# Two pairs of gate and up units per SwiGLU by Strassen's seven block products

## The chip, the cores and the metric

The kernel runs on one core of one Trainium2 chip. The metric is the device time of one execution in microseconds (us), the median of several runs. A profile is one execution of its own, with a time of its own.

## What is computed

A decoder trunk of four layers over 256 tokens of width 1024, in fp32. Each layer adds half a SwiGLU, a token mixer with a memory attention, and another half SwiGLU to the stream `x`; so there are eight SwiGLUs.

```python
def rms_norm(x, g):
    xf = x.astype(jnp.float32)
    y = xf * lax.rsqrt(jnp.mean(xf * xf, axis=-1, keepdims=True) + EPS)
    return (y * g.astype(jnp.float32)).astype(x.dtype)

def swiglu(x, wg, wu, wd):
    return (jax.nn.silu(x @ wg) * (x @ wu)) @ wd
...
x += 0.5 * swiglu(rms_norm(x, ffn_norm[i, j]), w_gate[i, j], w_up[i, j], w_down[i, j])
```

`w_gate` and `w_up` are 1024 x 2816, `w_down` is 2816 x 1024.

## The kernel before

The 256 tokens are two tiles of 128 (t = 0 and 1). Each tile is a generator, `chain(t)`, that runs through the layers and takes one unit of weights each time it is sent one. A unit is up to 2 MB of weights. For a gate/up unit ("g") it is 1024 x 512: 256 gate columns beside 256 up columns; a SwiGLU has eleven of them. Its down units ("d") are 512 x 1024 each (the last one is half). `FFN_ORDER` gives the order: four g, then d, then g, g, d and so on. `plan` writes down the units (`self.units`) and the order in which the chains get them (`self.seq`); `both` gives a unit to tile 0 and then to tile 1.

Precision: each fp32 operand is parted into a high part `hi`, which is the operand copied to fp32r, and the rest `lo`. A product is three matmuls of 128x128 by 128x512, hi x hi, hi x lo and lo x hi (`mm3`, lines 228 to 230). A g unit for one tile has eight blocks of K, so 24 matmuls, into one PSUM bank (`project`, tile `pg`). Of a d unit, four blocks of K into two banks, also 24 (tile `acc`).

Weights: `fetch` (line 182) loads a unit by two DMAs of 1 MB on SP's queue into `raw`, which has three buffers. `split` queues four quarters a unit; each is a copy on ScalarE (`hi`, line 200) and a subtraction on VectorE (`lo`, line 201) of 128x1024 elements. `hi` and `lo` have nine buffers each (`HALVES`). `split_some` issues queued quarters, one or two at each `tick`, and all of a unit's before the unit is used. `run` is the loop over `self.seq`; behind each unit it calls `advance`, which fetches the unit three further on and queues the quarters of the one two further on. A tick stands in the middle of a product and after it.

After a g unit, ScalarE takes a tanh of the gate half (line 1070), VectorE makes the product h in two steps (1071, 1076), and two units together are turned by TensorE and parted again (1084 to 1086). The norm is not applied to the tokens ahead of the product: the columns of `x` are turned and multiplied by the gains (`norm_half`, lines 324 to 329), and 1/rms of a token enters as a scale of the product (`norm_stats`, `rstd`, `rh`, `r2`, computed by POOL from a sum of squares of line 336).

Buffers are tiles of tags: `a4` (nine of 4 KB a partition, used by the mixers and by `scr` of `norm_stats`), `a2` (14 of 2 KB), `a1` (ten of 1 KB). PSUM: four banks A (`acc`, mixers), two B (`pg`), two C (`pT`, all turning). The code only says in which order work is issued; a scheduler settles at build time in which order each engine takes it, among what is ready and has a buffer, earlier issued work first, and places the semaphores. Each engine then works in that fixed order.

Of the kernel before, what the change touches and what calls it, by code (L numbers as in the profile page):

```python
# [78 lines left out]
class Net:  # L79
    def __init__(self, ctx, tc, a, layers):  # L80
        self.tc, self.nc, self.a = tc, tc.nc, a
        self.layers = layers

        def pool(name, **k):
            return ctx.enter_context(tc.tile_pool(name=name, bufs=1, **k))

        self.cp, self.wp, self.ap, self.sp = pool("const"), pool("weights"), pool("act"), pool("small")
        self.ps = pool("psum", space=PSUM)
        self.units, self.raw, self.parts = [], {}, {}
        self.n_fetch = self.n_split = 0  # L90
        self.seq, self.due, self.queue, self.memkv = [], [], [[], []], {}
        self.ticks = 0
        self.joint, self.open = [], []
        self.st, self.splits = [{}, {}], []
        self.plan()

# [29 lines left out]
    def plan(self):  # L126
        a = self.a

        def ffn(i, j):
            for kind, u in FFN_ORDER:  # L130
                if kind == "g":
                    self.units.append(("w", [a["gu"][i, j, u, 0], a["gu"][i, j, u, 1]], None))
                elif u < 5:
                    self.units.append(("w", [a["dn"][i, j, 2 * u], a["dn"][i, j, 2 * u + 1]], None))
                else:
                    self.units.append(("w", [a["dn"][i, j, 10]], None))

        def memory(i):
            self.units.append(("w", [a["memT"]], None))
            self.units.append(("w", [a["mkv"][i, 0], a["mkv"][i, 1]], i))  # L140
            self.seq.append((len(self.units) - 2, 2))

        def both(n):
            self.seq += [(n, 0), (n, 1)]

        for j, i in enumerate(self.layers):
            n = len(self.units)
            ffn(i, 0)
            for u in range(n, len(self.units)):
                both(u)  # L150
            if j == 0:
                memory(i)
            kind = i % 3
            names = {0: ["ret"] * 5, 1: ["dsa0", "dsa1", "dsa2", "dsa2"],
                     2: ["nsa0", "nsa0", "nsa0", "nsa1", "nsa2", "nsa3"]}[kind]
# [12 lines left out]
            self.seq += [(n - 2, 0), (n - 1, 0), (n - 2, 1), (n - 1, 1)]  # L168
            ffn(i, 1)
            for u in range(n, len(self.units)):  # L170
                both(u)

    def fetch(self):
        u = self.n_fetch
        if u >= len(self.units):
            return
        self.n_fetch += 1
        self.raw[u] = []
        for ap in self.units[u][1]:
            n = ap.shape[1]  # L180
# [1 line left out]
            self.nc.sync.dma_start(r, ap)  # L182
            self.raw[u].append(r)

    def split(self):

        nc, u = self.nc, self.n_split
        if u >= len(self.units):
            return
        self.n_split += 1  # L190
        self.parts[u] = []
        gain = self.units[u][2]

# [52 lines left out]
    def tick(self):  # L246
# [13 lines left out]

    def push(self, key, t, first, second=None):

        i = len(self.joint)
        while i and self.joint[i - 1][0] > key:
            i -= 1
        self.joint.insert(i, (key, t, first, second))

    def step(self):

        if self.joint and len(self.open) < 2:  # L270
            key, t, first, second = self.joint[0]
# [3 lines left out]
            self.joint.pop(0)  # L275
            first()
            if second is not None:
                self.open.append((t, second))
# [14 lines left out]
    def flush(self, t):  # L293
        due, self.due = self.due, []
        for n, fn, x in due:
            if x in (None, t):
                fn()
            else:
                self.due.append((n, fn, x))
        while any(o[0] == t for o in self.open) or any(j[1] == t for j in self.joint):  # L300
            self.step()
        while self.queue[t]:
            self.queue[t].pop(0)()
# [10 lines left out]
    def norm_half(self, t, g, b, st):  # L314
# [10 lines left out]
        for k in range(4):  # L325
# [3 lines left out]
            nc.vector.scalar_tensor_tensor(lo[:, c], p[:, k], gain, hi[:, c].bitcast(F32),  # L329
                                           op0=OP.mult, op1=OP.subtract)  # L330

    def norm_stats(self, t, st):
# [721 lines left out]
    def ffn(self, t, g, st):  # L1054
# [4 lines left out]
        for kind, ui in FFN_ORDER:  # L1059
            u = yield  # L1060
            if not H:
                s, r, rh, r2 = st["n"]
            if kind == "g":
                if u == 0:
                    p = self.first[t]
                else:
# [3 lines left out]
                nc.scalar.activation(th, p[:, :256], AF.Tanh, scale=rh)  # L1070
# [5 lines left out]
                nc.vector.scalar_tensor_tensor(hs, th, r2, p[:, 256:], op0=OP.mult, op1=OP.mult)  # L1076
# [12 lines left out]
            else:  # L1089
# [4 lines left out]
                for cb in range(2):  # L1094
# [6 lines left out]
                    if nd == 5:  # L1101
# [2 lines left out]
                        if g is None:  # L1104
                            nc.scalar.dma_start(self.a["out"][t * 128:(t + 1) * 128, cb * 512:cb * 512 + 512], xs)
                        else:
                            self.norm_half(t, g, cb, st)
                    if cb == 0:
                        self.tick()
                nd += 1  # L1110
# [19 lines left out]
    def opening(self):  # L1130
# [52 lines left out]
        def gained(t, b, p):  # L1183
            w = self.t2([128, 4, 128], "xg")
            nc.vector.tensor_mul(w, p, self.gains[:, g, 4 * b:4 * b + 4, None].to_broadcast([128, 4, 128]))
            return w

        def parted(t, b, w):
# [4 lines left out]
        def block(k, p):  # L1193
            hi, lo = self.st[0]["s"]
            gain = self.gains[:, g, k:k + 1]
            nc.scalar.activation(hi[:, k], p[:, k], AF.Copy, scale=gain)
            nc.vector.scalar_tensor_tensor(lo[:, k], p[:, k], gain, hi[:, k].bitcast(F32),
                                           op0=OP.mult, op1=OP.subtract)
            halve(k, 1)

        pt = turned(0, 0)
        self.idle(4)
        for k in range(2):
# [33 lines left out]
    def chain(self, t):  # L1237
# [3 lines left out]
        for i in self.layers:  # L1241
# [12 lines left out]
                xs = X[:, cb * 512:cb * 512 + 512]  # L1254
                nc.vector.tensor_add(xs, acc, xs)
            for b in range(2):
                self.norm_half(t, 2 * i + 1, b, st)
            self.norm_stats(t, st)
            yield from self.ffn(t, None if i == self.layers[-1] else 2 * i + 2, st)

    def run(self):
# [40 lines left out]
        for n, (u, t) in enumerate(self.seq):  # L1302
            self.split_some(0, u + 1 if t == 2 else u)
            try:
                chains[t].send(u)
            except StopIteration:
                pass
            self.tick()
# [100 lines left out]
```

## Time and profile before

| | |
|---|---|
| median of 3 runs | 2052.04 us (2051.94 to 2052.83) |
| the profiled execution's own time | 2050.38 us |
| its span, first to last instruction | 2048.6 us |
| TensorE, VectorE, ScalarE, POOL busy | 2029.6, 1250.7, 1015.5, 161.6 us |
| read from HBM | 349.07 MB |

The engines are PE (TensorE's matmuls; PEld is its loading of weights, which overlaps), DVE (VectorE), ACT (ScalarE), POOL (GpSimd) and SP, which only issues DMAs. A SwiGLU takes about 188 us of TensorE, eight of them some 1500 of the 2049 us; between them lie the mixers and the output projections. A matmul's duration in the trace contains its pipeline, so neighbours overlap; the pitch is the distance of starts.

### The profile page before, as it was taken

What the parts mean: (1) busy time and instruction counts of PE and PEld (TensorE: products, weight loads), DVE (VectorE), ACT (ScalarE), POOL (GpSimd) and SP (SyncE); (2) the same over time, 40 slices, a digit from 0 to 9 for tenths busy, and PEclk for the clock granted to TensorE, in tenths of its full rate; (3) what the DMA queues carried; (4) which work ended last, traced back from release to release, by engine and by line L of the source; (5) the groups of instructions that cost most, each with busy time, mean ns of one, the idle gap of its engine ahead of it and who ended that gap; (6) DMA issues with size and microseconds to landing.
All of it is one profiled execution on the core that took longest, in us unless ns stands there. A gap on an engine that the chain in (4) does not pass through costs nothing.

```text
span 2048.6 us, 25033 instructions
## 1 busy us (share of the span) xinstructions
PE 2029.6 (99%) x9662; PEld 1653.0 (81%) x9662; DVE 1250.7 (61%) x1912; ACT 1015.5 (50%) x1494; POOL 161.6 (8%) x285
## 2 busy tenths in 40 slices
PE   9999999999999999999999999999999999999999
PEld 6888777888888887888888877878888888778887
DVE  7556756555655687755665576765556656657553
ACT  6445555444544555544554455554445444546442
POOL 1000311000000122000000023210000000300000
PEclk9999999999999999999999999999999999999999
DMA  8454535455455423545445443134545545435451
GB/s 311 173 205 162 192 113 207 171 189 196 170 182 192 164 100 122 206 170 200 183 167 205 169 179 134 65 124 182 205 165 185 199 171 205 146 123 187 182 195 73
DMA packets 50854, 351.73 MB, mean 172 GB/s; under 512 B 5808, under 2 KB 6224, under 8 KB 9904
## 3 DMA queue, kind: packets, MB, share of 16 engines
q1 hardware_dynamic: 49392, 347.76, 46.5%
q10 hardware_dynamic: 1152, 1.97, 0.3%
q8 instruction: 76, 1.25, 0.2%
q0 software_dynamic: 192, 0.41, 0.1%
q14 instruction: 42, 0.34, 0.1%
HBM read 349.07 MB, written 1.05 MB: 171 GB/s over the span
## 4 chain that ended last, share of the span: by engine, by line
PE 94%; DVE 2%; POOL 1%; ACT 1%; issue 1%; DMA 1%; SPq 0%; ACTq 0%; DVEq 0%; POOLq 0%
PE pg L228 15%; PE pg L230 15%; PE pg L229 15%; PE acc L228 8%; PE acc L229 8%; PE acc L230 8%; PE p L228 3%; PE p L230 3%; PE p L229 3%; PE pT L1084 2%; PE pT L374 1%; PE po L228 1%; PE po L229 1%; PE po L230 1%; PE pT L324 1%; DVE lo L201 1%
## 5 line engine op out<-in xcount | busy, mean ns | idle before, releaser
L201 DVE TENSOR_TENSOR lo<-raw,hi 128x1024 fp32r<-128x1024 f32 (+2 forms) x644 | 775.0, 1221 | 353.8 <-ACT hi L200 336.8
L200 ACT ACTIVATE hi<-raw 128x1024 fp32r<-128x1024 f32 (+2 forms) x644 | 662.7, 1049 | 362.5 <-PE acc L230 201.6
L228 PE MATMUL pg<-hi,sh 128*128 128x512 f32 x1408 | 554.8, 394 | 2.7 <-ACT hi L1169 1.7
L229 PE MATMUL pg<-lo,sh 128*128 128x512 f32 x1408 | 549.0, 390 | 1.1 <-DVE lo L1170 1.0
L230 PE MATMUL pg<-hi,sl 128*128 128x512 f32 x1408 | 549.6, 390 | 0.0
L228 PEld LDWEIGHTS pg<-hi,sh 128*128 128x128 f32 x1408 | 264.4, 188 | 56.7 <-ACT hi L1169 2.2
L229 PEld LDWEIGHTS pg<-lo,sh 128*128 128x128 f32 x1408 | 264.6, 188 | 56.4 <-DVE lo L1170 3.2
L230 PEld LDWEIGHTS pg<-hi,sl 128*128 128x128 f32 x1408 | 264.3, 188 | 56.2 <-DVE sl L1191 0.4
L228 PE MATMUL acc<-hi,hTh 128*128 128x512 f32 x704 | 281.5, 400 | 0.0
L229 PE MATMUL acc<-lo,hTh 128*128 128x512 f32 x704 | 279.1, 396 | 0.0
L230 PE MATMUL acc<-hi,hTl 128*128 128x512 f32 x704 | 277.6, 394 | 0.0
L1070 ACT ACTIVATE th<-pg,rh 128x256 f32<-128x256 f32 x176 | 83.8, 476 | 323.4 <-PE pg L230 323.0
L1071 DVE SCALAR_TENSOR_TENSOR th<-th,pg 128x256 f32<-128x256 f32 x176 | 73.7, 419 | 211.5 <-ACT th L1070 211.5
L230 PEld LDWEIGHTS acc<-hi,hTl 128*128 128x128 f32 x704 | 132.3, 188 | 30.8 <-DVE hTl L1086 0.2
L228 PEld LDWEIGHTS acc<-hi,hTh 128*128 128x128 f32 x704 | 132.3, 188 | 30.0 <-ACT hTh L1085 1.3
L229 PEld LDWEIGHTS acc<-lo,hTh 128*128 128x128 f32 x704 | 132.4, 188 | 28.1
L228 PE MATMUL p<-hi,sh 128*128 128x512 f32 (+4 forms) x320 | 125.2, 391 | 0.3 <-DVE dq_b L356 0.3
L230 PE MATMUL p<-hi,sl 128*128 128x512 f32 (+4 forms) x320 | 121.1, 379 | 0.0
L229 PE MATMUL p<-lo,sh 128*128 128x512 f32 (+4 forms) x320 | 120.9, 378 | 0.0
L1085 ACT ACTIVATE hTh<-pT 128x512 fp32r<-128x512 f32 (+1 forms) x96 | 53.2, 554 | 79.6 <-PE pT L1084 79.6
L1076 DVE SCALAR_TENSOR_TENSOR h<-th,r,pg 128x256 f32<-128x256 f32 x176 | 84.6, 481 | 6.4
L309 POOL TENSOR_SCALAR rstd_m<-ss 128x1 f32<-128x1 f32 x24 | 10.0, 416 | 986.4 <-ACT scr L336 986.3
(292 smaller groups left out, 1812.5 us busy)
## 6 DMA issues: line engine op xcount, KB each, us to landing
raw<-gu SPq DMA_DIRECT2D x174, 1024.0 KB, 4.8
raw<-dn SPq DMA_DIRECT2D x88, 1024.0 KB, 4.8
raw<-ret SPq DMA_DIRECT2D x20, 1024.0 KB, 4.8
raw<-wout SPq DMA_DIRECT2D x16, 1024.0 KB, 4.8
raw<-mkv SPq DMA_DIRECT2D x8, 1024.0 KB, 4.8
raw<-nsa SPq DMA_DIRECT2D x6, 1024.0 KB, 4.9
raw<-memT SPq DMA_DIRECT2D x4, 1024.0 KB, 4.9
raw<-dsa SPq DMA_DIRECT2D x4, 768.0 KB, 4.3
```

The lines of the kernel that those rows point to most:

```text
L200: nc.scalar.activation(hi, src, AF.Copy)
L201: nc.vector.tensor_sub(lo, src, hi.bitcast(F32))
L228: mm(out, ah, bh, start=start, stop=False)
L229: mm(out, ah, bl, start=False, stop=False)
L230: mm(out, al, bh, start=False, stop=stop)
L324: nc.tensor.transpose(p[:, k], self.X[t][:, c * 128:(c + 1) * 128], self.ident)
L374: nc.tensor.transpose(p[:, k, :rows], s, self.ident[:rows, :rows])
L1070: nc.scalar.activation(th, p[:, :256], AF.Tanh, scale=rh)
L1071: nc.vector.scalar_tensor_tensor(th, th, 1.0, p[:, :256], op0=OP.add, op1=OP.mult)
L1076: nc.vector.scalar_tensor_tensor(hs, th, r2, p[:, 256:], op0=OP.mult, op1=OP.mult)
L1084: nc.tensor.transpose(c[:, k], h[:, k * 128:k * 128 + 128], self.ident)
L1085: nc.scalar.activation(hl[0][:, :n], c[:, :n], AF.Copy)
```

## The change

Units 4 and 5, and units 8 and 9, of every SwiGLU are multiplied together, for both tiles, as one product of a 2 x 2 block matrix (rows: the two tiles; columns: the two halves of K) with a 2 x 2 block matrix of weights (rows: the halves of K, each one raw tensor of 1 MB; columns: the two units). Strassen's form in Winograd's order takes seven block products of 4 blocks of K instead of eight. It needs sums of token blocks (`sums`, `ops` s1 to s4, once per SwiGLU) and of weights: t1 = b12 + b11 and t3 = b12 + b22 are made by loading b12 and then letting POOL issue a DMA that adds the other tensor onto it; t2 = t1 + b22 and t4 = t1 + b21 are made by VectorE in place. Each of the seven is parted in two quarters as before. The four results need sums of products in PSUM or SBUF (`s1`, `s2`, `s3`).

Since the two tiles' blocks are added, they must have one scale: tile 1's columns are multiplied by the ratio of the two tiles' 1/rms (`ratio`, a matmul with the identity that spreads it over partitions). For that `norm_kept` keeps the columns after the gains in `w` (tag `a2`); it takes the place of `norm_half` ahead of every SwiGLU, not ahead of the mixers. `scr` goes from `a4` to `a2` in bf16. The list `joint` of before is now called `jobs`. The opening, which is written in a fixed order, gets one more multiplication of a half by the gains.

```diff
+JOINT = (4, 8,)
...
         def both(n):
-            self.seq += [(n, 0), (n, 1)]
+            self.seq += [(n, 3)] if self.units[n][0] == "j" else [(n, 0), (n, 1)]
...
+    def fetch_joint(self, u):
+        nc = self.nc
+        b11, b21, b12, b22 = self.units[u][1]
+        half = lambda ap, q: ap[:, 1024 * q:1024 * q + 1024]
+        raw = self.raw[u] = {}
+        def plain(name, ap):
+            raw[name] = self.wp.tile([128, 2048], F32, name="raw", tag="raw", bufs=3)
+            nc.sync.dma_start(raw[name], ap)
+        def start(name):
+            raw[name] = [self.t4([128, 1024], "sum") for _ in range(2)]
+            for q in range(2):
+                nc.sync.dma_start(raw[name][q], half(b12, q))
+        def add(name, ap):
+            for q in range(2):
+                nc.gpsimd.dma_start(raw[name][q], half(ap, q), accum_op=OP.add)
+        plain("b11", b11)
+        start("t1")
+        add("t1", b11)
+        plain("b22", b22)
+        start("t3")
+        add("t3", b22)
+        plain("b21", b21)
+
+    def split_joint(self, u):
...
+        def quarter(name, src, q, plus):
+            x = half(src, q)
+            if plus:
+                nc.vector.tensor_add(x, x, half(plus, q))
+            hi = self.wp.tile([128, 1024], F32R, name="hi", tag="hi", bufs=HALVES)
+            lo = self.wp.tile([128, 1024], F32R, name="lo", tag="lo", bufs=HALVES)
+            nc.scalar.activation(hi, x, AF.Copy)
+            nc.vector.tensor_sub(lo, x, hi.bitcast(F32))
+            parts[name].append((hi, lo))
+        for name, src, plus in (("b11", "b11", None), ("t1", "t1", None), ("t2", "t1", "b22"), ("t3", "t3", None),
+                                ("b21", "b21", None), ("t4", "t1", "b21"), ("b22", "b22", None)):
+            for q in range(2):
+                self.splits.append((u, lambda name=name, src=src, q=q, plus=plus: quarter(name, src, q, plus)))
...
+        if self.extra:
+            self.extra.pop(0)()
...
+    def norm_kept(self, t, g, b, st):
...
+        w = st["w"][b] = self.t2([128, 4, 128], "xg")
+        nc.vector.tensor_mul(w, p, self.gains[:, g, c, None].to_broadcast([128, 4, 128]))
+        hi, lo = [x[:, c] for x in st["s"]]
+        nc.scalar.activation(hi, w, AF.Copy)
+        nc.vector.tensor_sub(lo, w, hi.bitcast(F32))
+
+    def sums(self):
...
+        self.extra += [ratio, lambda: scale(w10), lambda: scale(w11), first, lambda: parted("a22", w11), third, second,
+                       fourth]
+
+    def joint(self, u, chains):
...
+        def product(bank, a, name, first):
+            mm = nc.tensor.matmul
+            for k in range(4):
+                bh, bl = [x[:, k % 2 * 512:k % 2 * 512 + 512] for x in parts[name][k // 2]]
+                mm(bank, a[0][:, k], bh, start=first and k == 0, stop=False, skip_group_check=True)
+                mm(bank, a[0][:, k], bl, start=False, stop=False, skip_group_check=True)
+                mm(bank, a[1][:, k], bh, start=False, stop=k == 3, skip_group_check=True)
+                if k == 1:
+                    self.tick()
+        n0 = self.st[0]["n"]
+        A = self.pB("pg")
+        product(A, half(0), "b11", True)
+        s1 = self.t2([128, 512], "s1")
+        nc.scalar.activation(s1, A, AF.Copy)
+        B = self.pB("pg")
+        product(B, both("s2"), "t2", True)
+        s2 = self.t2([128, 512], "s2")
+        nc.vector.tensor_add(s2, B, s1)
+        C = self.bank("pj", "C")
+        product(C, both("s1"), "t1", True)
+        product(B, both("s3"), "t3", False)
+        s3 = self.t2([128, 512], "s3")
+        nc.vector.tensor_add(s3, B, s1)
+        product(A, half(1), "b21", False)
+        chains[0].send((A, n0))
+        nc.vector.tensor_sub(s3, C, s3)
+        product(B, both("a22"), "t4", False)
+        nc.vector.tensor_add(s1, B, s1)
+        chains[1].send((s1, n0))
+        chains[1].send((s3, n0))
+        product(C, both("s4"), "b22", False)
+        nc.vector.tensor_sub(s2, C, s2)
+        chains[0].send((s2, n0))
+
     def norm_stats(self, t, st):
-        scr = self.t4([128, 1024], "scr")
+        scr = self.t2([128, 1024], "scr", BF)
...
+                if t and ui == 0:
+                    self.sums()
```

## Rows read from the trace of the kernel before

**Rows 1.** The page: busy shares, TensorE's granted clock in 40 slices, DMA share.

```profile
PE 2029.6 (99%) x9662; PEld 1653.0 (81%) x9662; DVE 1250.7 (61%) x1912; ACT 1015.5 (50%) x1494; POOL 161.6 (8%) x285
...
PEclk9999999999999999999999999999999999999999
DMA  8454535455455423545445443134545545435451
```

**Rows 2.** The page: chain that ended last, by engine.

```profile
PE 94%; DVE 2%; POOL 1%; ACT 1%; issue 1%; DMA 1%; SPq 0%; ACTq 0%; DVEq 0%; POOLq 0%
```

**Rows 3.** TensorE's waits, longest: us in total, times, longest.

```profile
PE pT L501 <- POOL mk L496: 2.8, 3, 1.4
```

**Rows 4.** Timeline of TensorE: start us, us; first and last matmul of a product.

```profile
399.67 0.39 PE L228 MATMUL pg<-hi,sh 128*128 128x512 f32 x1
...
404.89 0.39 PE L230 MATMUL pg<-hi,sl 128*128 128x512 f32 x1
```

**Rows 5.** Busy time by stretch: two g units, then one d unit.

```profile
core 0: us, PE busy (x) PEld busy (x) DVE busy (x) ACT busy (x) POOL busy (x), PEclk, DMA share, GB/s
388.00:410.00 22.00, 22.00 (x101) 18.15 (x100) 14.11 (x17) 11.07 (x14) 0.00 (x0) 1.00 0.55 197
410.00:422.00 12.00, 12.00 (x56) 9.76 (x55) 5.00 (x7) 4.22 (x7) 0.00 (x0) 1.00 0.43 166
```

**Rows 6.** Timeline of TensorE in a mixer: fp32 matmuls, two passes each.

```profile
276.65 0.49 PE L609 MATMUL ro<-rv,rA 128*128 128x128 f32 x2
277.07 0.49 PE L608 MATMUL ro<-state,rqT 64*128 64x128 f32 x2
```

**Rows 7.** Instruction groups, shapes apart: busy us, mean ns | idle before, releasers.

```profile
L201 DVE TENSOR_TENSOR lo<-raw,hi 128x1024 fp32r<-128x1024 f32 x620 | 751.5, 1230 | 339.1 <-ACT hi L200 322.3
L200 ACT ACTIVATE hi<-raw 128x1024 fp32r<-128x1024 f32 x620 | 642.8, 1057 | 344.2 <-PE acc L230 199.0 <-PE pg L230 121.3 <-PE p L230 12.2
L329 DVE SCALAR_TENSOR_TENSOR sl<-pT,gains,sh 128x128 fp32r<-128x128 f32 x176 | 56.2, 346 | 26.7 <-ACT sh L328 25.8
L1085 ACT ACTIVATE hTh<-pT 128x512 fp32r<-128x512 f32 x80 | 47.2, 590 | 70.5 <-PE pT L1084 70.5
L1103 DVE SCALAR_TENSOR_TENSOR x<-acc,x 128x512 f32<-128x512 f32 x32 | 22.0, 689 | 17.5 <-PE acc L230 17.4
```

**Rows 8.** Timelines of ScalarE and VectorE at a down unit's end; idle before.

```profile
420.05 3.91 ACT L200 ACTIVATE hi<-raw 128x1024 fp32r<-128x1024 f32 x4 [5.66 <-PE acc L230]
...
421.14 4.63 DVE L201 TENSOR_TENSOR lo<-raw,hi 128x1024 fp32r<-128x1024 f32 x4 [6.03 <-ACT hi L200]
```

**Rows 9.** Timeline of TensorE: two accumulations taken in turn.

```profile
504.18 0.40 PE L229 MATMUL acc<-lo,hTh 128*128 128x512 f32 x1
504.41 0.40 PE L228 MATMUL acc<-hi,hTh 128*128 128x512 f32 x1
504.65 0.39 PE L230 MATMUL acc<-hi,hTl 128*128 128x512 f32 x1
```

**Rows 10.** DMA issues: count, KB each, median us to landing.

```profile
raw<-gu SPq DMA_DIRECT2D x2, 512.0 KB, 7.0
...
ga<-ngain POOLq DMA_DIRECT2D x1, 256.0 KB, 5.8
```

**Rows 11.** Timeline of SP's queue: loads of raw.

```profile
388.52 0.33 SPq L182 DMA_DIRECT2D raw<-dn  x1
390.80 17.87 SPq L182 DMA_DIRECT2D raw<-gu  x4
```

**Rows 12.** Timeline of POOL in the middle of a SwiGLU.

```profile
617.59 0.10 POOL L682 MEMSET dv<- 128x2 f32 x1 [92.28 <-DVE h L1076]
617.84 0.79 POOL L1028 DMA_DIRECT2D ga<-dgain  x1 [0.15 <-issue]
```

**Rows 13.** Busy time by stretch: the mixers of the second and third layer.

```profile
708.00:828.00 120.00, 118.27 (x662) 96.21 (x661) 95.33 (x239) 69.83 (x134) 27.39 (x44) 1.00 0.34 122
1205.00:1378.00 173.00, 168.76 (x1038) 138.30 (x1037) 115.40 (x262) 93.04 (x178) 45.49 (x67) 1.00 0.31 108
```

More of the change, by code (lines that the diff above doesn't have):

```diff
@@ L177, in fetch @@
         self.n_fetch += 1
+        if self.units[u][0] == "j":
+            self.fetch_joint(u)
+            return
         self.raw[u] = []
@@ L190, in split @@
         self.n_split += 1
+        if self.units[u][0] == "j":
+            self.parts[u] = {}
+            self.split_joint(u)
+            return
         self.parts[u] = []
@@ L261, in push @@
     def push(self, key, t, first, second=None):
-        i = len(self.joint)
-        while i and self.joint[i - 1][0] > key:
+        i = len(self.jobs)
+        while i and self.jobs[i - 1][0] > key:
             i -= 1
-        self.joint.insert(i, (key, t, first, second))
+        self.jobs.insert(i, (key, t, first, second))
     def step(self):
-        if self.joint and len(self.open) < 2:
-            key, t, first, second = self.joint[0]
+        if self.jobs and len(self.open) < 2:
+            key, t, first, second = self.jobs[0]
             if second is None and any(o[0] == t for o in self.open):
@@ L274, in step @@
                 return
-            self.joint.pop(0)
+            self.jobs.pop(0)
             first()
@@ L299, in flush @@
                 self.due.append((n, fn, x))
-        while any(o[0] == t for o in self.open) or any(j[1] == t for j in self.joint):
+        while any(o[0] == t for o in self.open) or any(j[1] == t for j in self.jobs):
             self.step()
@@ new lines, in sums, with ratio, scale, parted @@
+    def sums(self):
+        nc = self.nc
+        (w00, w01), (w10, w11) = self.st[0].pop("w"), self.st[1].pop("w")
+        ops = self.ops = {}
+        two = lambda x: x.rearrange("p a b -> p (a b)")
+        k = {}
+        def ratio():
+            q = self.ts(1, "ratio")
+            nc.vector.reciprocal(q, self.st[0]["n"][1])
+            nc.vector.tensor_mul(q, q, self.st[1]["n"][1])
+            rb = self.t1([128, 128], "rb")
+            nc.vector.tensor_copy(rb, q.to_broadcast([128, 128]))
+            k["R"] = self.pC("pR")
+            nc.tensor.matmul(k["R"][:, 0], rb, self.ident, start=True, stop=True)
+        def scale(w):
+            nc.vector.tensor_mul(w, w, k["R"][:, 0, None, :].to_broadcast([128, 4, 128]))
+        def parted(name, w):
+            o = ops[name] = self.t4([128, 2, 4, 128], "op", F32R)
+            nc.scalar.activation(o[:, 0], w, AF.Copy)
+            nc.vector.tensor_sub(o[:, 1], w, o[:, 0].bitcast(F32))
+        def first():
+            k["w"] = self.t2([128, 4, 128], "xs")
+            nc.vector.tensor_sub(two(k["w"]), two(w10), two(w11))
+            parted("s1", k["w"])
+        def third():
+            nc.vector.tensor_sub(two(w10), two(w00), two(w10))
+            parted("s3", w10)
+        def second():
+            nc.vector.tensor_sub(two(k["w"]), two(k["w"]), two(w00))
+            parted("s2", k["w"])
+        def fourth():
+            nc.vector.tensor_add(two(w01), two(w01), two(k["w"]))
+            parted("s4", w01)
+        self.extra += [ratio, lambda: scale(w10), lambda: scale(w11), first, lambda: parted("a22", w11), third, second,
+                       fourth]
@@ new lines, in joint @@
+    def joint(self, u, chains):
+        nc = self.nc
+        while self.extra:
+            self.extra.pop(0)()
+        parts, ops = self.parts[u], self.ops
+        s0 = self.st[0]["s"]
+        both = lambda n: (ops[n][:, 0], ops[n][:, 1])
+        half = lambda b: (s0[0][:, 4 * b:4 * b + 4], s0[1][:, 4 * b:4 * b + 4])
+        def product(bank, a, name, first):
+            mm = nc.tensor.matmul
+            for k in range(4):
+                bh, bl = [x[:, k % 2 * 512:k % 2 * 512 + 512] for x in parts[name][k // 2]]
[28 more added lines that the diff above has]
+        chains[0].send((s2, n0))
@@ L1256, in chain @@
             for b in range(2):
[L1257 removed]
+                self.norm_kept(t, 2 * i + 1, b, st)
             self.norm_stats(t, st)
@@ L1304, in run @@
             try:
-                chains[t].send(u)
+                if t == 3:
+                    self.joint(u, chains)
+                else:
+                    chains[t].send(u)
             except StopIteration:
```

34 lines of the change are left out of this document (29 added, 5 removed).

## The prediction, made before the result was known

> **What bounds the kernel now.** I read the page's shares first: TensorE is busy 99% of the span at the full granted clock in every slice, VectorE 61%, ScalarE 50%, the DMA engines about half [rows 1]. The chain that ended last is 94% TensorE, most of it the gate and up products (pg) and the down products (acc) [rows 2]. Then the list of what TensorE waited for: its longest entry is 2.8 us in total [rows 3]. So inside the SwiGLUs nothing but TensorE's own stream sets the end, and an instruction taken out of it is worth its pitch, as long as the stream stays fed. The pitch is read from starts, since durations of pipelined matmuls overlap (0.39 us shown): 23 steps from 399.67 to 404.89 us, 0.227 us a matmul [rows 4]. How much spare time the feeders have is read from one stretch of two gate/up units and the down unit behind them: in 22 + 12 us VectorE works 14.11 + 5.00 us, ScalarE 11.07 + 4.22 us, the DMA engines 0.55 and 0.43 of the time [rows 5].
>
> **What is removed.** A pair of units for both tiles is 2 x 2 x 24 = 96 matmuls; seven block products of 4 x 3 are 84. Two pairs in each of eight SwiGLUs are 16 joints: 16 x 12 = 192 matmuls x 0.227 = **43.6 us**, all on the path. A joint's products then take 84 x 0.227 = 19.1 us, each product 2.73 us.
>
> **What is added on TensorE.** Per SwiGLU one fp32 128x128 matmul for the ratio of the two tiles' norms; such a one takes 0.42 us of the stream (276.65 to 277.07) [rows 6]: 8 x 0.42 = 3.4 us. Transposes keep their number.
>
> **What is added beside it.** Per joint VectorE gets six more quarter splits (14 for 8), four sums of weights and five sums of products: 10 x 1.22 + 5 x 0.69 = 15.6 us; ScalarE six copies and s1, 6 x 1.06 + 0.59 = 6.9 us [rows 7]. The eight steps of sums() are, by the same rows, about 7.5 us of VectorE and 3 us of ScalarE per SwiGLU, spread over units 1 and 2, where VectorE is idle a third of the time [rows 5]; I cost them at nothing, and if that cover were gone a step would cost its 0.7 us. VectorE rises to (1251 + 16 x 15.6 + 8 x 7.5) / 2025 = 77%: not the bound on average. But a joint and its down unit now hold 19.1 + 15.6 = 34.7 us of VectorE work in 19.1 + 12 = 31 us, so it works them off with its lead, and I go through the joint with a clock.
>
> The lead: nine hi/lo buffers. At the end of a down unit its four are freed within the last 2 us, and at once four splits run back to back, 3.91 us on ScalarE and 4.63 us on VectorE, 1.16 us each, after 6 us of idleness [rows 8]. So the splits are held by buffers, not by speed. Let the joint start at 0. Five of its 14 quarters are ready. VectorE starts the next four at about -0.9; five more follow as products 1 to 3 free theirs, and all stand ahead of the sums of products in the program: 9 x 1.16 ends at 9.5, then s2 (0.69) at 10.2. Product 4 adds onto the bank that s2 reads, so it waits for s2. In program order it would be due at 8.2 (a stall of 2.1 us with the semaphore); but product 5 uses the other bank, and if TensorE takes it first, product 4 is due at 10.9 and nothing stalls. TensorE's order in the trace is not program order: a hi/lo step of one down product is followed by the first step of another before its own third [rows 9], so the swap is likely. The two sums for t4 need t2's and b21 only; one fits before the joint, where VectorE idles, the other pushes s2 by 1.16 to 11.4: a stall of 0.5. Behind product 4, product 6 waits for s3 in the same way, some 0.9 us, unless the down unit's matmuls fill in. Bounds per joint: 0 and 3.7 (both t4 sums inside and one quarter of the down unit ahead of s2: 10.2 + 2.3 + 1.2 + 0.1 - 10.9 = 2.9; and 0.8 for s3). I take **0.6**, near the lower end, because the row with 6 us of idleness says that VectorE uses every early chance. 16 x 0.6 = 9.6 us.
>
> **The transfers.** A joint loads seven times 1 MB for four, two of them as accumulating transfers issued by POOL; no row of before shows such a one. The nearest: 512 KB on SP landed in 7.0 us in the crowded opening, 256 KB issued by POOL in 5.8 us [rows 10]. So 6 to 14 us for a pair of halves. They have time: the four loads of the units that start at 422 and 433 are issued from 390.8 to 408.7, some 24 to 31 us ahead, and the second load of the down unit at 410 at 388.5 [rows 11], and the sums use other buffers than raw. First load 7 us, POOL 0.7 us a transfer (0.79 for one) [rows 12], then the pair; t2 is wanted at 2.7 and takes 3.5 us to add and split. From -31 there are 31 + 2.7 - 3.5 - 8.4 = 22 us for the first pair: I cost it at nothing; past 22 us each us counts, 16 times. Also POOL's queue: behind a waiting accumulation only the rstd steps of the next norm and the mixers' small work stand, half a SwiGLU away. The Trainium skill ("DMA: Bandwidth & Descriptors", Anatomy of one DMA) fits transfers of this path as 2.0 us plus bytes over 436 GB/s; an estimate by that page is 3.2 us for 512 KB, which would leave the sum as it is. No row here shows whether the adding slows it.
>
> **The rest.** norm_kept replaces four small VectorE steps of 0.346 us by two of 0.69 per half [rows 7]: no change of load, and its latency lies beside the other tile's products. The opening gets one more 0.69 us step on VectorE within its hand-written order: 0.7 us. The four buffers of the sums come from the nine that the mixers use too, and instructions are placed far ahead of their turn: a memset and a DMA of the second layer's mixer stand at 617 us, some 85 us before that mixer [rows 12]. So the sums of a second SwiGLU can hold buffers at the end of a mixer. Mixers have little slack (VectorE 95 of 120 us in one, TensorE short by 1.7 of 120 and 4.2 of 173 us) [rows 13]. Between 0 and about 5 us a mixer; I take 0.5 x 4 = 2 us, since the overlap is only the tail.
>
> **Sum**, against the profiled run's own 2050.4 us: 2050.4 - 43.6 + 3.4 + 9.6 + 0.7 + 2.0 = 2022.5. The median of the runs is 1.7 above that run: **2024 us**.
>
> **Rivals.**
> Late VectorE (slower than before): splits and weight sums stand ahead of s2 and s3, the stall is the upper 3.7 us a joint: 2022.5 - 9.6 + 59 + 1.7 = 2074. It decides from (43.6 - 3.4 - 0.7 - 2) / 16 = 2.3 us a joint. For it: 34.7 us of work in 31. Against it: the idle 6 us before the four splits. Chance 0.15.
> Late accumulation: a pair takes 30 us, not 14: 8 us a joint, 2022.5 + 128 + 1.7 = 2152, slower from 24 us on. For it: 9 MB in 31 us where 6 MB in 34 us had a share of 0.5, so 0.84 while it lasts, and more if adding costs. Against it: two stretches together, 15 MB for 12, come to 0.66. Chance 0.08. The Trainium skill (same page, Issuing engines are not separate DMA queues) speaks for this one: transfers from POOL get no engines of their own and mix with SP's. The trace of before has no stretch with both.
> Mixers starved of buffers: 4 x 4 us instead of 2: 2038; 0.12.
> The product is not shorter: TensorE keeps program order and loses the 2.1 us: 2022.5 + 24 + 1.7 = 2048, no difference that counts; 0.05.
> Forecast as above, stalls 0 to 1.3 us: 0.60.
>
> **Numbers.** The lower end is no stall and no loss in mixers, 2012.5, less 1 us for pitches as long as acc's and 1.5 for the runs' spread: 2010. Upwards the range takes in the starved mixers, the program order and the lower third of the late VectorE, up to 2056; left out are late accumulation and the worse part of late VectorE, about 0.18. A measurement of this kernel tells 0.2%, 4 us, from no change. Faster: 0.60 + 0.12 + 0.03 = 0.75; within: 0.07; slower: 0.18.
>
> **What would show it.** TensorE with 192 matmuls fewer and 16 more for the ratio (two passes each); a joint of 84 matmuls in 19 to 20 us. A wait of product 4 on s2 (a VectorE sum) in the list of TensorE's waits: under 1 us each if I am right, above 2.3 us if late VectorE is. A wait of a split or of a weight sum on an accumulating transfer would show late accumulation. A TensorE share below 97% in the mixers would show starvation. VectorE near 77%. The forecast is wrong if TensorE's pitch in a joint is not 0.227 us or if its idle time in the SwiGLUs is above 40 us in all.

## The result: 2108.1 us, slower by 2.7%

| | before | after |
|---|---|---|
| median, us | 2051.99 | 2108.09 (2104.33 to 2109.68) |
| ratio | | 1.0272, 95% interval 1.0259 to 1.0285 |
| profiled run: own time, span, us | 2050.4, 2048.6 | 2109.7, 2107.9 |
| mean granted TensorE clock | 1.00 | 0.985 |

The forecast was 2024 us, faster. The page of the changed kernel (busy shares, clock and DMA share in 40 slices, two DMA queues with packets, MB and share of the engines' time, the chain, three of the DMA issues), against [rows 1, 2, 10]:

```profile
PE 2028.5 (96%) x9486; PEld 1628.5 (77%) x9486; DVE 1520.9 (72%) x2209; ACT 1114.2 (53%) x1562; POOL 227.7 (11%) x349
...
PEclk9999999999999999999999999999999999999999
DMA  7855535865683533684577443137744774436843
...
q1 hardware_dynamic: 56304, 364.54, 47.2%
q0 software_dynamic: 9408, 33.97, 8.3%
...
PE 74%; DMA 12%; DVE 8%; ACT 3%; issue 2%; POOL 1%; SPq 0%; ACTq 0%; DVEq 0%; POOLq 0%
...
sum<-gu SPq DMA_DIRECT2D x64, 512.0 KB, 7.6
sum<-gu POOLq DMA_DIRECT2D x64, 512.0 KB, 11.5
```

The 176 TensorE instructions fewer (192 off, 16 passes for the ratio) are there. But the chain, 94% TensorE in [rows 2], is now 12% DMA and 8% VectorE, and the clock's mean has fallen although no slice of the page shows it. q0, the queue of the adding transfers, takes 8.3 / 33.97 against 47.2 / 364.54: 1.9 times the engine time of a plain load for each MB. What TensorE waited for (us in total, times, longest), against [rows 3]:

```profile
PE acc L292 <- ACT hi L264: 34.9, 8, 5.7
PE pT L1262 <- DVE h L1254: 20.7, 15, 5.1
```

The first is one wait in each of the eight SwiGLUs, seven of 4.3 to 5.7 us and one of 0.8. Of the second, eight waits (13.6 us) stand behind a copy for which ScalarE had waited for a sum. Here is the second SwiGLU's, by stretch (busy time of each engine, granted clock, DMA share, GB/s); the first joint runs from 402 to 433, with the down unit's matmuls and the stall among its products:

```profile
core 0: us, PE busy (x) PEld busy (x) DVE busy (x) ACT busy (x) POOL busy (x), PEclk, DMA share, GB/s
389.00:402.00 13.00, 11.91 (x54) 9.48 (x53) 7.94 (x9) 4.92 (x7) 0.00 (x0) 1.00 0.61 166
402.00:416.00 14.00, 14.00 (x63) 11.52 (x62) 13.39 (x13) 9.26 (x11) 1.74 (x2) 1.00 0.71 186
416.00:422.00 6.00, 1.12 (x5) 0.57 (x3) 0.15 (x1) 0.96 (x1) 0.87 (x1) 0.97 1.04 295
422.00:428.00 6.00, 5.38 (x12) 3.92 (x13) 4.28 (x6) 1.51 (x4) 0.88 (x1) 0.50 1.03 371
428.00:442.00 14.00, 13.60 (x63) 10.82 (x62) 11.01 (x16) 8.96 (x12) 0.00 (x0) 0.98 0.82 279
```

TensorE stands from 416.7 to 422.1, and in the 6 us behind that it gets half the clock, the lower of its two levels (1.2 of 2.4 GHz): 12 matmuls are recorded where 26 would go. Followed back through the timelines of POOL, ScalarE, TensorE, VectorE and SP (start us, us; idle time before, releaser):

```profile
375.39 0.96 POOL L214 DMA_DIRECT2D sum<-gu  x1 [26.05 <-DMA sum<-gu]
378.18 0.88 POOL L214 DMA_DIRECT2D sum<-gu  x1 [1.83 <-PE pg L294]
...
390.05 1.06 ACT L236 ACTIVATE hi<-sum 128x1024 fp32r<-128x1024 f32 x1 [2.42 <-DMA sum<-gu]
391.01 0.46 ACT L1248 ACTIVATE th<-pg,rh 128x256 f32<-128x256 f32 x1
...
393.50 0.44 PE L1262 MATMUL pT<-ident,h 128*128 128x128 f32 x2 [1.09 <-DVE h L1254]
...
401.88 0.39 PE L474 MATMUL pg<-hi,sh 128*128 128x512 f32 x1
...
407.95 1.22 DVE L233 TENSOR_TENSOR sum<-sum,raw 128x1024 f32<-128x1024 f32 x1
409.09 0.69 DVE L488 TENSOR_TENSOR s<-pg,s 128x512 f32<-128x512 f32 x1
...
409.20 0.33 SPq L193 DMA_DIRECT2D raw<-dn  x1
...
409.29 1.06 ACT L236 ACTIVATE hi<-sum 128x1024 fp32r<-128x1024 f32 x1 [2.89 <-DVE sum L233]
...
421.04 2.00 ACT L264 ACTIVATE hi<-raw 128x1024 fp32r<-128x1024 f32 x2 [6.89 <-DMA raw<-dn]
...
422.15 0.80 PE L292 MATMUL acc<-hi,hTh 128*128 128x512 f32 x1 [5.03 <-ACT hi L264]
...
426.99 0.63 PE L474 MATMUL pg<-hi,op 128*128 128x512 f32 x1
427.42 0.63 PE L475 MATMUL pg<-lo,op 128*128 128x512 f32 x1
```

The last two starts are 0.43 us apart where [rows 4] had 0.227. The load that was waited for is the second of the down unit in the middle of the joint. It is issued at 409.20, 7.3 us into the joint, as soon as VectorE's last sum for t4 (407.95 to 409.17) gives back the buffer of b21. The corresponding load before was issued 21 us ahead of its unit [rows 11]. It then takes

```profile
DMA to landing us min/median/max: 11.7/11.7/11.7
```

where the page's median of the down loads is 4.9 us: the second joint's sums are fetched and added in the same stretch, and the DMA share is over 1 as the view counts it.

To add up: distances of neighbouring TensorE starts above 0.6 us, each less the usual 0.227, sum to 83.6 us in the trace after and 15.2 before, 68.4 more. The clock's mean would give (1 - 0.985) x 2108 = 31.6 us, but of the 61.5 us at half clock, in ten stretches, some 18 lie in these gaps; the rest costs half its length, about 22. So -43.6 + 3.4 + 68.4 + 22 = 50; measured, span against span, 59.3. The other 9 us are in no long gap and are not assigned.

### The profile page after: what moved, and what is told of

The parts are those of the page before. It is cut to its first block, busy times and chain, and to the rows that moved or that the text cites. A ratio compares the mean times of both kernels' runs of the same rounds, so it can differ in the third digit from the quotient of the medians.

```text
span 2107.9 us, 25369 instructions
## 1 busy us (share of the span) xinstructions
PE 2028.5 (96%) x9486; PEld 1628.5 (77%) x9486; DVE 1520.9 (72%) x2209; ACT 1114.2 (53%) x1562; POOL 227.7 (11%) x349
## 2 busy tenths in 40 slices
DMA packets 66988, 402.11 MB, mean 191 GB/s; under 512 B 7600, under 2 KB 8016, under 8 KB 28080
## 3 DMA queue, kind: packets, MB, share of 16 engines
q1 hardware_dynamic: 56304, 364.54, 47.2%
q0 software_dynamic: 9408, 33.97, 8.3%
HBM read 399.40 MB, written 1.05 MB: 190 GB/s over the span
## 4 chain that ended last, share of the span: by engine, by line
PE 74%; DMA 12%; DVE 8%; ACT 3%; issue 2%; POOL 1%; SPq 0%; ACTq 0%; DVEq 0%; POOLq 0%
PE pg L292 8%; PE pg L294 8%; PE pg L293 8%; PE acc L293 7%; PE acc L294 6%; PE acc L292 6%; DMA sum<-gu 5%; DVE lo L237 4%; DMA raw<-gu 3%; PE p L292 3%; DMA raw<-dn 3%; PE p L293 3%; PE p L294 3%; DVE lo L265 2%; PE pT L1262 2%
## 5 line engine op out<-in xcount | busy, mean ns | idle before, releaser
L265 DVE TENSOR_TENSOR lo<-raw,hi 128x1024 fp32r<-128x1024 f32 (+3 forms) x516 | 615.6, 1217 | 175.1 <-ACT hi L264 168.5
L264 ACT ACTIVATE hi<-raw 128x1024 fp32r<-128x1024 f32 (+3 forms) x516 | 527.1, 1046 | 273.0 <-DMA raw<-gu 79.0
L292 PE MATMUL pg<-hi,sh 128*128 128x512 f32 x896 | 354.8, 396 | 4.4 <-ACT hi L1347 3.4
L293 PE MATMUL pg<-lo,sh 128*128 128x512 f32 x896 | 350.7, 391 | 0.7 <-DVE lo L1348 0.7
L294 PE MATMUL pg<-hi,sl 128*128 128x512 f32 x896 | 349.8, 390 | 0.0
L292 PE MATMUL acc<-hi,hTh 128*128 128x512 f32 x704 | 286.0, 410 | 34.9 <-ACT hi L264 34.9
L236 ACT ACTIVATE hi<-sum 128x1024 fp32r<-128x1024 f32 x128 | 132.3, 1057 | 165.4 <-PE acc L294 88.9
L237 DVE TENSOR_TENSOR lo<-sum,hi 128x1024 fp32r<-128x1024 f32 x128 | 154.2, 1226 | 77.6 <-ACT hi L236 75.9
L293 PEld LDWEIGHTS pg<-lo,sh 128*128 128x128 f32 x896 | 168.5, 188 | 35.4 <-DVE lo L1348 2.5
L294 PEld LDWEIGHTS pg<-hi,sl 128*128 128x128 f32 x896 | 168.2, 188 | 35.6 <-DVE sl L1370 0.4
L237 DVE TENSOR_TENSOR lo<-raw,hi 128x1024 fp32r<-128x1024 f32 x96 | 114.9, 1226 | 18.9 <-ACT hi L236 18.9
## 6 DMA issues: line engine op xcount, KB each, us to landing
sum<-gu POOLq DMA_DIRECT2D x64, 512.0 KB, 11.5
```

Of the source, the lines that this page charges most:

```text
L236: nc.scalar.activation(hi, x, AF.Copy)
L237: nc.vector.tensor_sub(lo, x, hi.bitcast(F32))
L264: nc.scalar.activation(hi, src, AF.Copy)
L265: nc.vector.tensor_sub(lo, src, hi.bitcast(F32))
L292: mm(out, ah, bh, start=start, stop=False)
L293: mm(out, ah, bl, start=False, stop=False)
```

## Experiments

Two theories stood first. Contention: the adding transfers hold the DMA engines, and whatever is loaded beside them lands late. Raw buffers: a joint holds the three buffers of plain loads too long, so that the next load is issued late. "Gaps" below are the sum of TensorE's long start distances, as above (15.2 before, 83.6 after), with the mean clock of the profiled run; the expectation of e12 counts them a little otherwise. All ratios are to the kernel before.

### e1, e2: one joint of the two

```diff
-JOINT = (4, 8,)
+JOINT = (4,)      # e1; (8,) in e2
```

> Only units 4 and 5 are a joint (JOINT = (4,)); units 8 and 9 are multiplied as before the change. Theory (contention): in the changed kernel the second joint's sums are loaded while the first joint runs, and take the DMA engines from the second load of the down unit behind it (landing 11.7 us for 4.8). Without a second joint that load lands in 5 to 6 us, the wait of 4.3 to 5.7 us behind the first joint falls under 1 us, the granted clock stays at 1.0 there, and the time is 2052 less 8 x 2.73 plus 8 x 0.42 plus some stalls: 2033 to 2042. Rival (raw buffers): the load is late because three raw buffers are all held by the joint until t4's sum; then the wait and the half clock stay, about 8 us a SwiGLU, and the time is 2085 to 2105.

> Only units 8 and 9 are a joint (JOINT = (8,)). Both theories: the second joint showed no wait in the changed kernel, so 8 x (2.73 - 0.42) = 18.5 us are gained, less what the sums' steps and early transfers disturb: 2033 to 2040. If its sums, now loaded during the first units of the SwiGLU, disturb other loads there, more: contention expects at most 3 us a SwiGLU, 2060. The rival of raw buffers expects 2033 to 2040.

e1: 2059.4 us, ratio 1.0031 (1.0019 to 1.0043), gaps 29.2, clock 0.997. e2: 2040.4, ratio 0.9941 (0.9927 to 0.9956), gaps 16.0, clock 0.998. The wait behind the first joint is gone from e1, though the joint's own loads and buffers are as they were: it takes the second joint's sums beside it. The same lines of e1, the joint's first matmul, the down unit's second load and its landing:

```profile
397.86 0.39 PE L474 MATMUL pg<-hi,sh 128*128 128x512 f32 x1
...
405.21 0.33 SPq L193 DMA_DIRECT2D raw<-dn  x1
...
DMA to landing us min/median/max: 4.7/4.7/4.7
```

The load is issued 7.35 us into the joint, as late as after the change (7.32), but lands in 4.7 us and not in 11.7. But e1 lies above what contention gave. TensorE waits ahead of the joint remain (12.3 us in 7 times, on h, each behind a sum that ScalarE waited for). The second joint alone is nearly free.

### e3: the second joint's sums start later

```diff
+                if self.second:
+                    nc.vector.tensor_copy(raw[name][q][:, :1], self.seen_h[:, :1])
                 nc.sync.dma_start(raw[name][q], half(b12, q))
```

> Both joints; the loads that begin the second joint's sums wait for a product h of unit 6 (one-element copy by VectorE into each sum tile), so that they start some 40 us later, behind the first joint and its down unit. Contention: the wait behind the first joint falls under 1 us, no half clock there, and the time is 2015 to 2030. Rival (raw buffers): the wait stays 4 to 6 us, 2090 to 2110.

2099.2 us, 1.0220 (1.0193 to 1.0248), gaps 72.3, clock 0.986. Held back until unit 6's h, the sums no longer run beside the first joint, and its stall is gone: the down load, still issued 7.4 us into the joint, lands in 4.8 us. In its place TensorE stands 4.0 to 5.5 us in each SwiGLU, ahead of the second joint: ScalarE stands in front of a sum that is still being added, with the tanh of the next unit behind it. Neither theory's number was right: sums started early collide, sums started late are late.

### e4: the same transfers, not added

```diff
-                nc.gpsimd.dma_start(raw[name][q], half(ap, q), accum_op=OP.add)
+                nc.gpsimd.dma_start(raw[name][q], half(ap, q))
```

> POOL's 64 transfers are plain copies: b11 and b22 overwrite b12 in the sums instead of being added to it, so the joints' products are other ones; bytes from HBM, issue and order are as in the changed kernel. Per MB the queue of the adding transfers had 8.3% of the engines for 33.97 MB, SP's 47.2% for 364.54, so adding costs 1.9 times a copy. Contention: POOL's transfers land in 6 to 8 us instead of 11.5, the share of their queue falls to 4 to 5%, the wait behind the first joint falls to 0 to 3 us, and the time is 2030 to 2075. Rival (raw buffers): the wait falls only by what t4's sum comes earlier, at most 2 us, and the time is 2080 to 2105.

2062.9 us, 1.0050 (1.0033 to 1.0066), gaps 47.2, clock 0.990. q0 takes 4.6% for its 33.97 MB, about as much per MB as a plain load, and its transfers land in 8.7 us, not 11.5. So adding costs about 1.8 times the engine time and 2.8 us a transfer, and through that 45 us of the kernel. The wait behind the first joint shrinks (34.9 to 19.1 us) and does not go. In the second SwiGLU the down load lands in 9.6 us, for 11.7, and TensorE waits 2.9 us, for 5.0: of the 7 us over e1's 4.7, the transfers beside this load cost 4.8 and the adding in them 2.2.

### e5: four buffers for plain loads

```diff
-HALVES = 9
+HALVES = 8
...
-            r = self.wp.tile([128, n], F32, name="raw", tag="raw", bufs=3)
+            r = self.wp.tile([128, n], F32, name="raw", tag="raw", bufs=4)
```

> As the changed kernel, with four raw buffers of 1 MB for four (and eight pairs of split halves for nine, to make room). The contention theory (the adding transfers slow every transfer beside them, however early it was issued): an earlier issue puts the down load into the same stretch, the sums still land late, the time stays within 15 us of 2108 (2090 to 2120). The raw-buffer theory (the load behind the first joint is only issued late): the 5 us wait behind the first joint falls to under 1 us in each of the eight SwiGLUs, 40 us and the clock lost behind it come back: 2045 to 2070.

2042.6 us, 0.9959 (0.9943 to 0.9974), gaps 36.3, clock 0.998. One pair of halves less made the room, so two things differ. 65 us came back, more than the rival asked for, with the sums as slow as ever (11.5 us). SP's timeline and the stretches of the same SwiGLU:

```profile
379.80 0.33 SPq L193 DMA_DIRECT2D raw<-dn  x1
...
402.00:408.00 6.00, 6.00 (x27) 4.62 (x26) 6.00 (x7) 6.00 (x7) 0.87 (x1) 1.00 0.95 248
408.00:414.00 6.00, 6.00 (x27) 4.87 (x27) 5.08 (x7) 1.04 (x3) 0.87 (x1) 1.00 1.05 344
414.00:420.00 6.00, 6.00 (x28) 4.81 (x26) 5.24 (x8) 4.61 (x6) 0.87 (x1) 1.00 1.04 364
```

The down load is issued at 379.80, 13 us ahead of the joint and not 7.3 us into it, and lands in 9.0 us. The DMA engines are as full in the joint as after the change, and TensorE does not notice. So full engines alone cost nothing there; they cost where a load has been issued too late to bear them. What is left are 16.4 us in 12 waits on h; 12.7 of them, eight waits, stand behind a late sum.

### e6, e8, e9: GpSimd makes the sums

```diff
-        start("t1")
-        add("t1", b11)
...
+        for q in range(2):
+            nc.sync.dma_start(raw["t1"][q], half(b12, q))
         plain("b22", b22)
-        start("t3")
-        add("t3", b22)
+        for q in range(2):
+            nc.gpsimd.tensor_add(raw["t3"][q], raw["t1"][q], half(raw["b22"], q))
+        for q in range(2):
+            nc.gpsimd.tensor_add(raw["t1"][q], raw["t1"][q], half(raw["b11"], q))
```

e8 is this with the second joint alone. e9 loads b12 into t3's tiles and makes t1 = b12 + b11 first, ahead of the load of b22.

> Both joints, but b12 is loaded once, by SyncE's queue, and GpSimd adds it to b11 and to b22 on the chip: four adds of 128x1024 a joint, by the rows of 128x256 at 0.77 to 1.34 us some 3 to 5 us each, 12 to 20 us of an engine that is 11% busy. No adding transfer is left, and a joint moves 4 MB for 6. The theory that the adding transfers cost the time (their engine time, and what waits for them): the 5 us waits are gone, TensorE's gaps over 0.6 us sum to under 30 us, granted clock 0.995 or more, 2015 to 2040. The rival that the order of the work is at fault (three buffers held by a joint, fourteen splits and six adds ahead of it in the queues of ScalarE and VectorE, whoever makes the sums): waits of 1 to 5 us in each SwiGLU remain, 2050 to 2100.

> Only the second joint, its sums made by GpSimd: 96 matmuls off for 192. With adding transfers this joint alone gave 2040.4. Adding-transfer theory: the sums of the second joint cost little already there, so 2033 to 2041, and above the kernel with both joints made by GpSimd (by some 15 us). Order-of-work rival: 2033 to 2041 too, but below the kernel with both joints.

> Both joints with GpSimd's sums as in e6, but t1 = b12 + b11 is made ahead of t3 = b12 + b22, so that the first sum no longer waits for the load of b22 and for two other adds of 2.5 us. The theory that the time is lost where ScalarE, whose work is taken in order, stands at the first half of a sum with the tanh of the next unit queued behind it: each 4 to 5 us wait of TensorE on h in e6 (16 of them, 63.5 us) shrinks by the two adds and the load it no longer waits for, 5 us and more, and most vanish; the clock comes back; 2030 to 2060. The rival that GpSimd's adds cost by what they take from VectorE (1362 ns for 1226 ns of a split's subtraction beside them): the waits stay at 3 us or more, 2095 to 2125.

e6: 2127.8 us, 1.0370 (1.0355 to 1.0386), gaps 89.7, clock 0.979. The theory that only the adding transfers cost time falls: there are none, and it is the slowest of all. e6's timelines of GpSimd, ScalarE and TensorE:

```profile
383.90 4.79 POOL L213 TENSOR_TENSOR sum<-sum,raw 128x1024 f32<-128x1024 f32 x2 [32.59 <-DMA raw<-gu]
388.64 5.78 POOL L215 TENSOR_TENSOR sum<-sum,raw 128x1024 f32<-128x1024 f32 x2
...
392.07 1.06 ACT L230 ACTIVATE hi<-sum 128x1024 fp32r<-128x1024 f32 x1 [4.08 <-POOL sum L215]
...
395.42 0.46 ACT L1242 ACTIVATE th<-pg,rh 128x256 f32<-128x256 f32 x1
...
399.15 0.69 PE L1256 MATMUL pT<-ident,h 128*128 128x128 f32 x2 [4.53 <-DVE h L1248]
```

GpSimd waits for b22, then needs 8 us to the first half of t1. ScalarE takes its work in order: it stands 4.08 us at that half, the tanh (th) behind it goes late, h goes late, TensorE stands 4.53 us. So whoever makes the sums, this queue hands the lateness on, and long before a product needs the sum. e8, one joint alone, shows it too: 2090.0 us, 1.0183 (1.0166 to 1.0200), gaps 50.8, against 2040.4 for e2; both theories had said 2033 to 2041.

e9: 2076.7 us, 1.0119 (1.0093 to 1.0146), gaps 61.0, clock 0.997. Taking b22 and two adds out of the way of t1 gave back 51 us, and the 4 to 5 us waits are gone; one of 7.8 us stands in the first SwiGLU, and its cause was not looked for. But the price is above the expected 2060, and the rival may have had part of it: VectorE and GpSimd get in each other's way. What that costs the kernel is not shown.

```profile
375.35 6.14 POOL L212 TENSOR_TENSOR sum<-sum,raw 128x1024 f32<-128x1024 f32 x2 [25.71 <-DMA sum<-gu]
...
375.79 6.79 DVE L259 TENSOR_TENSOR lo<-raw,hi 128x1024 fp32r<-128x1024 f32 x2
```

Two subtractions of VectorE take 6.79 us beside two adds of GpSimd, where two alone take 2.4 [rows 7]; by the groups, a split of the joint's raw halves takes 1715 ns on the mean, not 1226. The Trainium skill ("SBUF — State Buffer", Who interferes with whom) has it that a VectorE instruction with two inputs in SBUF contends with a GpSimd instruction that reads SBUF; these two rows agree.

### e7: VectorE makes the sums

```diff
-        start("t1")
-        add("t1", b11)
...
+        for q in range(2):
+            nc.sync.dma_start(raw["t1"][q], half(b12, q))
         plain("b22", b22)
-        start("t3")
-        add("t3", b22)
...
+            if name == "t1":
+                nc.vector.tensor_add(half("t3", q), x, half("b22", q))
+                nc.vector.tensor_add(x, x, half("b11", q))
```

> As the kernel whose sums GpSimd makes, but VectorE makes them, four more adds of 128x1024 at 1.23 us a joint, 16 x 4.9 = 79 us more of its time (72% of the span to 76%). The adding-transfer theory alone: 2015 to 2040, as with GpSimd. If VectorE becomes late ahead of the joints: waits of TensorE on its halves of 1 to 3 us at most joints, 2045 to 2080.

2027.5 us, 0.9882 (0.9867 to 0.9896), gaps 18.3, clock 1.00. Every long wait is gone, with three buffers. VectorE is 78% busy. The same lines as in e1:

```profile
391.14 0.40 PE L467 MATMUL pg<-hi,sh 128*128 128x512 f32 x1
...
398.49 0.33 SPq L193 DMA_DIRECT2D raw<-dn  x1
...
DMA to landing us min/median/max: 4.7/4.7/4.7
```

The down load is again issued 7.35 us into the joint, so late sums had not delayed it. It lands in 4.7 us, since no adding transfers and fewer bytes are beside it (351.74 MB in all, for 402.11), and TensorE does not wait for it. With e1 and e5 this settles the stall: a late issue alone does not make it, nor a slow landing alone; the two together do.

### e10, e11: a third joint

```diff
-JOINT = (4, 8,)
+JOINT = (4, 6, 8)
...
-        add("t1", b11)
...
             if plus:
-                nc.vector.tensor_add(x, x, half(plus, q))
+                nc.vector.tensor_add(x, half("t3", q) if name == "t1" else x, half(plus, q))
```

VectorE makes the sums here too, one add at the turn of each half; e11 has four raw buffers besides (and eight pairs of halves for nine).

> VectorE makes the sums, one add for each of t1 to t4's halves at its turn, and a third pair of units (6 and 7) is made a joint: 96 matmuls more are gone, 96 x 0.227 = 21.8 us below the two joints' 2027.5 if all else is hidden, 2004 to 2012. VectorE was busy 1250.7 us before and 1587.9 with two joints and its own sums, so with three about 1700 us of 2010, 85%, and more inside the SwiGLUs: if it is late there (the rival of the prediction, now with its cause), waits of TensorE on its halves or on h of 0.5 to 2 us a joint appear, 2012 to 2045. If the joint between two joints has its loads held by the three buffers: waits of 3 to 5 us and a clock below 0.995, 2060 to 2110.

> As the kernel with three joints, with four raw buffers of 1 MB and eight pairs of halves. If the three buffers hold its loads back: 15 us and more below it. If VectorE is what is late there, or nothing: within 5 us of it.

e10: 2094.0 us, 1.0204 (1.0170 to 1.0237), gaps 99.0, clock 0.997. e11: 2100.0, 1.0233 (1.0208 to 1.0257), gaps 94.8, clock 0.986. Two of TensorE's waits and two stretches of e10:

```profile
PE pg L465 <- DVE lo L227: 29.5, 17, 1.8
PE pg L464 <- DVE s L478: 20.4, 17, 1.2
...
420.00:460.00 40.00, 36.04 (x157) 27.89 (x156) 39.15 (x44) 22.88 (x28) 0.00 (x0) 1.00 0.47 171
460.00:500.00 40.00, 35.59 (x155) 27.69 (x154) 39.10 (x46) 23.65 (x28) 0.00 (x0) 1.00 0.41 155
```

VectorE works 78.25 of 80 us: it is the bound there, and buffers do not help: e10's time lies where I had put late loads, but e11 is no faster. This is the prediction's late VectorE, waits on halves and on the sums of products (s) included; with two joints (e7) the same 40 us stretches hold 31.23 and 33.90 us of it, and it hardly appears (one wait on s, 1.2 us). I had expected 2012 to 2045 for it, too little, since I took only waits and no lasting bound.

### e12: VectorE's sums and four buffers

```diff
-HALVES = 9
+HALVES = 8
...
-        add("t1", b11)
...
             if plus:
-                nc.vector.tensor_add(x, x, half(plus, q))
+                nc.vector.tensor_add(x, half("t3", q) if name == "t1" else x, half(plus, q))
...
-            r = self.wp.tile([128, n], F32, name="raw", tag="raw", bufs=3)
+            r = self.wp.tile([128, n], F32, name="raw", tag="raw", bufs=4)
```

> Both remedies together: two joints, the sums made by VectorE one at each half's turn, and four raw buffers. If the two causes found (the load behind the first joint issued late for want of a buffer; the sums that ScalarE stands at) are the whole loss, each remedy alone already took away most of it and both together bring nothing more than the TensorE gaps that e7 kept above the kernel before (20.1 us for 15.4): 2020 to 2029. If a third cause is left that neither touched, as VectorE being near its limit inside the SwiGLUs, the time stays at e7's 2027.5 or rises a little, 2027 to 2040.

2022.3 us (2021.99 to 2022.45), 0.9859 (0.9842 to 0.9875), gaps 18.9, clock 0.999: the fastest, 86 us below the changed kernel. The 5 us below e7 are not assigned: each add also comes at its half's turn here. Its page and its longest wait of TensorE:

```profile
PE 1998.9 (99%) x9486; PEld 1615.4 (80%) x9486; DVE 1584.2 (78%) x2273; ACT 1113.8 (55%) x1562; POOL 170.1 (8%) x285
...
PE pT L664 <- POOL mk L659: 2.6, 2, 1.3
```

The longest wait is again the mixer's, as in [rows 3]. From the span of 2048.6: -43.6 + 3.4 + (18.9 - 15.2) + 1 for the clock = 2013 against a span of 2020.1; 7 us are in no long gap.

## Why the prediction was wrong

The step that failed is the transfers: "I cost it at nothing". Three parts of it:

- "the sums use other buffers than raw". They do, but the joint's plain loads do not. I read in [rows 11] that the down unit's second load goes out 21 us ahead, and did not ask what holds its buffer once a joint stands before it: b21 is needed until the last sum for t4, late in the joint. It went out at 409.20, 7.5 us before its turn, and so it does, 7.3 to 7.4 us into this joint, with three buffers in e1, e3, e4 and e7. Where it landed in 4.7 or 4.8 us (e1, e3, e7) that cost nothing; beside the second joint's sums it took 11.7. This wait, 34.9 us, and the seven of ten stretches at half clock behind it are the largest part of the loss, and not in the sum at all. A fourth buffer (e5) takes 65 us off the changed kernel, sums made by VectorE (e7) 81: either remedy takes the same wait away.
- "past 22 us each us counts". The limit was taken from the product that needs t2. What comes first is ScalarE's queue: the copies of a sum's halves stand ahead of the tanh of units before the joint. In the second SwiGLU the first pair's adding transfers were issued from 375.39 and had landed by 390.0: 14.6 us, just above my 6 to 14 and inside the 22. My 31 us ahead was near (368.3 to 401.9). Even so ScalarE stood 2.42 us at the second half, the tanh behind it went late and TensorE stood 1.09 us. Eight such waits are 13.6 us after the change.
- The adding itself. 1.8 times the engine time per MB and 11.5 us to landing, against 8.7 plain (e4). The late-accumulation rival, 0.08 at 2152 us, was right that adding slows these transfers, but not in how that costs: it reckoned with 30 us a pair against the turn of t2, and the pair above took 14.6. With the loads issued earlier (e5) the same transfers leave the kernel faster than before. The estimate of 3.2 us by the Trainium skill's fit ("DMA: Bandwidth & Descriptors", Anatomy of one DMA) is far from both measured landings. What the page states of engines shared by all queues (Issuing engines are not separate DMA queues) agrees: a 1 MB load on SP's queue took 11.7 us beside the sums and 4.9 on the median.

The clock was not in the sum either. Where TensorE stood 4 to 6 us it went on at half its clock for about 6 us: some 22 us in the changed kernel, a third of the 68.4 us of the gaps themselves. I wrote that each us past the limit counts once, and should have let a long stand count more.

Point by point, what held. 192 matmuls came off, and their pitch was 0.227 to 0.23 us in the undisturbed stretches. The ratio's price and the 77% of VectorE were near (72%; 78% with all sums on it). Neither the stall of product 4 on s2 (9.6 us in the sum) nor that on s3 appeared: no such wait is among TensorE's waits after the change. In the joint above s2 ended 7.9 us in (409.09 + 0.69), not 10.2, ahead of product 4's turn in program order, and no swap was needed. Late VectorE was not what decided; it did with a third joint (e10). The mixers were not starved: none of the waits listed after the change is theirs beyond those that stood there before. Two signs on the prediction's list came true: idle time in the SwiGLUs above 40 us, and copies that wait on an adding transfer (ScalarE, 22.8 us in 9 times). Without the two late things, the sum of the prediction (2022.5, 2024 with the offset to the median) is what e12 measured, partly by luck: the 9.6 us for s2 that never came stand against small gaps that I had at nothing.

What stays open: the 9 us of the sum that no long gap holds; what of e7's gain is the adding and what the fewer bytes; and what the pair of halves taken away in e5 and e12 did.

## What to carry to other kernels

When a change keeps data longer, find whose next load needs that buffer, and read its issue and its turn from the trace before: its lead is what the change spends. Then compare the lead that is left with the landing time beside the new transfers, not the one of before. A sum that is "wanted" by a late product is wanted much earlier by an engine that takes its work in order, so count slack to the place in that queue, and count a TensorE gap of several us at about one and a half. An add that an engine with room does in 1.2 us was cheaper there than in a transfer (e7); on GpSimd, at 2.4 us and late, it was not (e6).

## What the runs showed of the hardware

An adding transfer of 512 KB took 11.5 us to landing and 1.8 to 1.9 times the engine time of a plain one per MB. DMA engines at a share of 1.04 to 1.05 (344 to 364 GB/s) did not slow TensorE when its data was there (e5). A 1 MB load on SP's queue landed in 4.7 us without the second joint's transfers beside it (e1), in 9.6 with them (e4) and in 11.7 when they added. After gaps of 4 to 6 us TensorE ran at half its clock for about 6 us. Many gaps, 99 us in all but no wait over 2.1 us, left its mean at 0.997 (e10). In e11 no wait was longer than 2.4 us, but in each SwiGLU two starts in a row came 2.4 to 2.8 us apart, and it went on at half clock there: 0.986. A GpSimd add and a VectorE subtraction of 128x1024 beside each other took 3.1 and 3.4 us (e9), for 2.4 (e8) and 1.22 apart.
